# The recurrent layer's mixing weights split during the feed-forward layer before it and kept in DRAM; two elementwise steps on other engines

## The chip, the cores and the metric

One core of a Trainium2 chip runs the whole program. The metric is device time in microseconds (us) from the first to the last instruction of one execution, with what the runtime puts around it; the median of three runs is compared.

## What is computed

Two blocks of two layers each act on 512 tokens of width 1024. The change touches the second block: its first feed-forward layer (width 2816) and the recurrent layer after it (`odd_mixer`). Cut to those:

```python
def swiglu(x, w_gate, w_up, w_down):
    return (silu(x @ w_gate) * (x @ w_up)) @ w_down

def odd_mixer(xn, w_in, w_out, ...):
    z = xn @ w_in                                    # 1024 -> 2048
    h = rglru_mixer(z[..., :1024], ...)
    return (h * gelu(z[..., 1024:])) @ w_out

def rglru_mixer(xb, ...):
    xc = causal_conv(xb, conv_w) + conv_b            # 4 taps
    gate_r = sigmoid(xc @ w_r + b_r)                 # 4 diagonal blocks of 256
    gate_i = sigmoid(xc @ w_i + b_i)
    log_a = -8 * gate_r * softplus(-lam)
    a, mult = exp(log_a), sqrt(-expm1(2 * log_a))
    return scan(h[t] = a[t] * h[t-1] + mult[t] * (gate_i * xc)[t])

for layer in range(2):
    x = x + rms_norm(mixer(rms_norm(x)))             # even_mixer, odd_mixer
    x = x + rms_norm(swiglu(rms_norm(x)))
```

## The kernel before

Activations lie with channels on the 128 partitions and the 512 tokens along the row. Every product is made in three parts: a weight block of 128 outputs by 1024 inputs and the activations are each split into a high half (rounded to the matmul's type) and a low half (the rest), and `product` (L288) adds high by high, high by low and low by high: 24 matmuls of 512 columns a block. `weights` (L269) gets one block: SyncE (SP) starts a load of 512 KB into a raw tile `wp_r`, ScalarE (ACT) copies it into `wp_h`, and a subtraction into `wp_l` runs on VectorE (DVE) unless an engine is named. There are three raw tiles and four of each half. `firsts` (L299) does the first three blocks of a layer together, one half of the tokens at a time, so that it can begin while the norm before it is still running; it splits its weights on GpSimd (POOL).

`ffn` (L1755) runs over 22 pairs of blocks (gate and up), in three groups of 6, 8 and 8. A pair's two products are scaled by the norm (`g_g`, `g_u`), go through Silu, are multiplied on POOL, and are split into `h_h` and `h_l`; after each group come eight blocks of the down weights, and after the last group a norm and the residual (`po_a`, `po_r`, `g_ff`, `res_x`), whose outputs `act_h` and `act_l` the next layer reads.

`odd_mix` (L1646) is the recurrent layer's mixing, in four blocks b of two channel tiles each. `conv(b)` takes two blocks of `w_in` (m = 0 to 7), multiplies by the norm into `xb`, makes the first tap with bias (`ts`, L1677) and adds three taps (`stt`), then splits the result into `o_h` and `o_l`. `gates(b)` multiplies by the block of `w_rg` and takes tanh. `states(b)` makes the decay and the input of the recurrence (`o_mu`, `o_a`, `o_tr`, `o_ti`) and scans it into `o_u`; in it, the product of r0 and i0 runs on POOL. `gate(b)` takes two more blocks of `w_in` (m = 8 to 15) into `o_z`, and `gated(b)` applies gelu, multiplies and splits into `b_h` and `b_l`, which `out_products` (L339) multiplies by the output weights. The blocks for `conv` and the four `w_rg` have their low halves made on POOL, those for `gate` on DVE. The norm of the layer is summed into `res_acc` and needed by the first `xb`.

The text of the kernel gives the order of dependences only: the library that builds the program puts each engine's instructions, and SP's transfers, in a queue of their own, an instruction as early as it reckons its operands and buffers free, ties by the order of the text. Each queue is then carried out strictly in that order.

Of the kernel before, what the change touches and what calls it, by code (L numbers as in the profile page):

```python
# [188 lines left out]
class Prog:  # L189
# [79 lines left out]
    def weights(self, ap, n=1024, eng=None, pool=None):  # L269

        pool = pool or self.wp
        raw = (pool if "r" in pool.tags else self.wp)("r", n)
        self.nc.sync.dma_start(out=raw, in_=ap)
        hi, lo = self.parts_of(pool, n)
        self.copy(hi, raw)
        self.sub(lo, raw, hi.bitcast(F32), eng)
        return hi, lo
# [1368 lines left out]
    def odd_mix(self, es, B):  # L1646
        nc, tc, xs, r = self.nc, self.tc, self.xs, self.rr
        A = Alloc(es, tc, "o7", {
            "sp2": (1, 8), "hb": (1, 16), "h": (4, L), "l": (4, L), "xb": (2, L + 3), "xc": (2, 1024),
            "tr": (2, 1024), "ti": (2, 1024), "a": (2, L), "mu": (2, L), "u": (2, 1024), "z": (2, 1024),  # L1650
        })
        ps = self.psum(mm=4, g=4)

        sp = self.sp
        sp2, hb = A("sp2"), A("hb")
        self.ts(sp2, sp, 2.0, ALU.mult)
        self.ts(hb[:, 0:8], self.vec("rg_b_r"), 0.5, ALU.mult)
        self.ts(hb[:, 8:16], self.vec("rg_b_i"), 0.5, ALU.mult)
        cw, cb = self.vec("rg_cw"), self.vec("rg_conv_b")

        def proj(m, eng=None):
            if m in first:
                return first[m][0]
            w = self.weights(self.I["w_od"][m], eng=eng or nc.gpsimd)
            px = ps("mm")
            self.product(px, w, xs, X)
            return px

        def conv(b):
            c2, parts = A("xc"), []  # L1670
            for i in range(2):
                m = 2 * b + i
                px = proj(m)
                xb, c = A("xb"), c2[:, i * L:(i + 1) * L]
                nc.gpsimd.memset(xb[:, 0:3], 0.0)
                self.mul(xb[:, 3:], px, r)
                self.ts(c, xb[:, 3:], cw[:, 4 * m + 3:4 * m + 4], ALU.mult, cb[:, m:m + 1], ALU.add)  # L1677
                for j in range(3):
                    self.stt(c, xb[:, j:j + L], cw[:, 4 * m + j:4 * m + j + 1], c, ALU.mult, ALU.add)
                parts.append(self.split(A, c))  # L1680
            return c2, parts

        us, ys = {}, []

        def gates(b, c2, parts):
            w = self.weights(self.I["w_rg"][b], eng=nc.gpsimd)
            tr, ti = A("tr"), A("ti")
            for i in range(2):
                m, s = 2 * b + i, slice(i * L, (i + 1) * L)
                for g, t in enumerate((tr, ti)):  # L1690
                    p = ps("g")
                    self.product(p, w, parts, X, k0=4 * g + 2 * i)
                    self.act(t[:, s], p, ACT.Tanh, scale=0.5, bias=hb[:, 8 * g + m:8 * g + m + 1])
            return tr, ti

        def states(b, c2, tr, ti):


            h, ts = A("u"), []
            for i in range(2):  # L1700
                m, s = 2 * b + i, slice(i * L, (i + 1) * L)
                u, w = A("mu"), A("a")
                self.act(u, tr[:, s], ACT.Tanh, scale=sp[:, m:m + 1], bias=sp[:, m:m + 1])
                self.act(w, tr[:, s], ACT.Exp, scale=sp2[:, m:m + 1], bias=sp2[:, m:m + 1])
                nc.scalar.activation(out=w, in_=w, func=ACT.Copy, scale=0.5, bias=0.5)
                ts.append((s, tr[:, s], ti[:, s], u, w))
            for s, r0, i0, u, w in ts:
                self.act(r0, u, ACT.Sqrt, scale=-1.0)
                self.stt(u, u, -1.0, w, ALU.add, ALU.mult)
                self.stt(w, u, 2.0, w, ALU.add, ALU.mult)  # L1710
                self.stt(i0, i0, 1.0, c2[:, s], ALU.add, ALU.mult)
                self.mul(r0, r0, i0, nc.gpsimd)
                self.mul(r0, r0, w)
                self.ts(w, w, 2.0, ALU.mult, -1.0, ALU.add)
                nc.vector.tensor_tensor_scan(out=h[:, s], data0=w, data1=r0, initial=0.0, op0=ALU.mult, op1=ALU.add)
            us[b] = h

        def gate(b):
            z = A("z")
            for i in range(2):  # L1720
                px = proj(8 + 2 * b + i, nc.vector)
                self.mul(z[:, i * L:(i + 1) * L], px, r)
            return z

        def gated(b, z, cuts):
            self.act(z, z, ACT.Gelu_apprx_tanh)
            hi, lo = self.parts_of(B)
            for s in cuts:
                self.mul(z[:, s], us[b][:, s], z[:, s])
                self.copy(hi[:, s], z[:, s])  # L1730
                self.sub(lo[:, s], z[:, s], hi[:, s].bitcast(F32))
            ys.extend((hi[:, s], lo[:, s]) for s in halves)

        halves, whole = (slice(0, L), slice(L, 2 * L)), (slice(0, 2 * L),)
        first = dict(enumerate(self.firsts(ps, [self.I["w_od"][m] for m in range(3)], xs)))
        self.rms(ps("g"))
        cs, zs = {0: conv(0), 1: conv(1)}, {}
        for b in range(3):
            t = gates(b, *cs[b])
            zs[b] = gate(b)  # L1740
            if b == 2:
                t3 = gates(3, *cs[3])
            states(b, cs[b][0], *t)
            if b < 2:
                cs[b + 2] = conv(b + 2)
            if b:
                gated(b - 1, zs[b - 1], whole)
        states(3, cs[3][0], *t3)
        zs[3] = gate(3)
        gated(2, zs[2], whole)  # L1750
        gated(3, zs[3], halves)
        return ys


    def ffn(self, l, last=None):  # L1755

        nc, tc, xs, r = self.nc, self.tc, self.xs, self.rr
        with ExitStack() as es:
# [5 lines left out]
            def proj(m):  # L1764
                w = self.weights(self.I[f"w_gu{l}"][m])
                px = ps("mm")
                self.product(px, w, xs, X)
                return px

            first = [px for px, _ in self.firsts(ps, [self.I[f"w_gu{l}"][m] for m in range(3)], xs)]  # L1770
            first.append(proj(3))
            self.rms(ps("z"))
            for a, b in ((0, 6), (6, 14), (14, 22)):
                hs = []
                for i in range(a, b):
# [11 lines left out]
                    self.copy(hi, t[0])  # L1787
                    self.sub(lo, t[0], hi.bitcast(F32))
                    hs.append((hi, lo))
                if l == a == 0:  # L1790
                    self.softplus()
                n = (b - a) * 128
                block = lambda m: self.I[f"w_d{l}"][m][:, a * 128:b * 128]
                if b < 22:
                    for m in range(8):
# [5 lines left out]
                        else:  # L1801
                            self.add(ff[m], ff[m], px)
                else:
                    pre, stats = (last, None) if last else self.prenorm(es, ps, "norm_mix_pre", l + 1)
                    use, done = self.postnorm(es, ps, "norm_ffn_post", l, pre, ff, last)
                    self.out_products(ps, block, hs, PARTS[:2], use, done, n=n, keep=4 if last else 3, spare=(H, 2))
# [65 lines left out]
```

## Time and profile before

| | us |
|---|---|
| median of 3 runs | 2132.29 (2127.01 to 2133.92) |
| the profiled execution | 2134.38 |
| its span, first to last instruction | 2132.6 |
| PE busy in it | 2045.8 (96%) |
| DVE, ACT, POOL busy | 1349.8, 911.0, 427.0 |

The second block's first feed-forward layer reads its first weights at about 1153 and runs to about 1560; the recurrent mixing goes on from there to about 1715, its output product to about 1750. Times in the trace are counted from the span's start. A line such as L250 is a helper's (`tt`), so steps are told apart by their tiles: `o_` are those of the recurrent mixing, `g_` and `h_` of the feed-forward layer, `wp_` weights, `po_` a norm after a product. PE is TensorE. An arrow `<-` in a wait names what ended it.

### The profile page before, as it was taken

The page shows a single profiled execution, that of the slowest core. Times are in us where ns is not written, and L with a number is a line of the kernel's source. Part 1 is how long each engine was busy: PE and PEld are TensorE (multiplying, and loading weights), DVE is VectorE, ACT ScalarE, POOL GpSimd, SP SyncE. Part 2 cuts the span into 40 slices and gives each one's busy share as a digit, 9 for nine tenths or more (in the row PEclk, how much of TensorE's full clock was granted, in tenths as well). Part 3 has the DMA queues.
Part 4 walks back from the last instruction along what each step waited for, and adds up shares of the span by engine and source line. Part 5 has one row for each costly group of instructions (what it writes and reads, how often), then busy time and mean ns, then how long its engine had stood idle before and what let it go on. Part 6 is the DMA issues. An engine that isn't in the chain of part 4 may idle for free.

```text
span 2132.6 us, 29872 instructions
## 1 busy us (share of the span) xinstructions
PE 2045.8 (96%) x11624; PEld 1740.2 (82%) x11624; DVE 1349.8 (63%) x2290; ACT 911.0 (43%) x1634; POOL 427.0 (20%) x403
## 2 busy tenths in 40 slices
PE   6999999999999999989999999999989799999997
PEld 4888888889888888888778888888877588888886
DVE  6775566786666665786665734535589886254455
ACT  2563343445433444455655533222356645322231
POOL 1111111354122221042112310101143322010011
PEclk9999999999999999999989999999999899999998
DMA  8344442321111111224423133333312232333231
GB/s 300 119 158 136 146 142 71 116 88 60 50 54 56 50 50 50 89 85 158 119 70 99 60 96 102 99 98 93 116 50 69 70 99 80 109 96 93 98 109 40
DMA packets 80142, 204.97 MB, mean 96 GB/s; under 512 B 19200, under 2 KB 28160, under 8 KB 80000
## 3 DMA queue, kind: packets, MB, share of 16 engines
q1 hardware_dynamic: 80000, 203.06, 30.1%
q8 instruction: 91, 1.49, 0.3%
q14 instruction: 51, 0.42, 0.1%
HBM read 188.87 MB, written 14.16 MB: 95 GB/s over the span
## 4 chain that ended last, share of the span: by engine, by line
PE 76%; DVE 13%; issue 5%; ACT 4%; POOL 1%; DMA 1%; SPq 0%; POOLq 0%; DVEq 0%; ACTq 0%
PE mm L313 56%; PE a L313 5%; PE mc L313 3%; PE x L313 2%; PE S L313 2%; DVE res_x L266 1%; PE s L313 1%; PE pt L651 1%; PE o L313 1%; DVE wp_l L250 1%; PE mc L425 1%; DVE o_xc L266 1%; DVE n_a L250 1%; ACT wp_h L244 1%; PE z L313 1%
## 5 line engine op out<-in xcount | busy, mean ns | idle before, releaser
L244 ACT ACTIVATE wp_h<-wp_r 128x1024 fp32r<-128x1024 f32 (+2 forms) x263 | 271.3, 1037 | 456.1 <-PE mm L313 263.4
L250 DVE TENSOR_TENSOR wp_l<-wp_r,wp_h 128x1024 fp32r<-128x1024 f32 (+1 forms) x236 | 326.9, 1388 | 108.7 <-ACT wp_h L244 108.6
L313 PE MATMUL mm<-act_h,wp_l 128*128 128x512 f32 (+1 forms) x1008 | 379.4, 376 | 12.0 <-DVE wp_l L250 10.2
L313 PE MATMUL mm<-act_l,wp_h 128*128 128x512 f32 (+1 forms) x1008 | 380.0, 377 | 1.9 <-POOL act_l L250 1.9
L313 PE MATMUL mm<-act_h,wp_h 128*128 128x512 f32 (+1 forms) x1008 | 379.8, 377 | 1.7 <-ACT wp_h L244 1.3
L313 PE MATMUL mm<-a_h,wp_h 128*128 128x512 f32 (+1 forms) x920 | 336.8, 367 | 5.5 <-ACT wp_h L244 3.3
L313 PE MATMUL mm<-a_h,wp_l 128*128 128x512 f32 (+1 forms) x920 | 329.8, 359 | 1.2 <-POOL wp_l L250 1.2
L313 PE MATMUL mm<-a_l,wp_h 128*128 128x512 f32 (+1 forms) x920 | 328.6, 358 | 0.9 <-DVE a_l L250 0.9
L313 PEld LDWEIGHTS mm<-act_h,wp_l 128*128 128x128 f32 x1008 | 194.0, 192 | 46.4 <-DVE wp_l L250 11.1
L313 PEld LDWEIGHTS mm<-act_l,wp_h 128*128 128x128 f32 x1008 | 193.6, 192 | 35.9 <-POOL act_l L250 2.6
L313 PEld LDWEIGHTS mm<-act_h,wp_h 128*128 128x128 f32 x1008 | 193.5, 192 | 34.7 <-ACT wp_h L244 1.8
L313 PEld LDWEIGHTS mm<-a_h,wp_h 128*128 128x128 f32 x920 | 174.1, 189 | 30.6 <-ACT wp_h L244 3.3
L313 PEld LDWEIGHTS mm<-a_l,wp_h 128*128 128x128 f32 x920 | 174.1, 189 | 25.9 <-issue 1.9
L313 PEld LDWEIGHTS mm<-a_h,wp_l 128*128 128x128 f32 x920 | 173.8, 189 | 24.6 <-POOL wp_l L250 1.4
L250 POOL TENSOR_TENSOR g_g<-g_g,g_u 128x512 f32<-128x512 f32 x44 | 61.1, 1390 | 549.3 <-DVE g_u L250 502.9
L313 PE MATMUL mm<-h_l,wp_h 128*128 128x512 f32 (+1 forms) x344 | 129.2, 376 | 0.6 <-DVE h_l L250 0.5
L313 PE MATMUL mm<-h_h,wp_h 128*128 128x512 f32 (+1 forms) x344 | 129.0, 375 | 0.3 <-ACT h_h L244 0.3
L313 PE MATMUL mm<-h_h,wp_l 128*128 128x512 f32 (+1 forms) x344 | 128.8, 374 | 0.0
L250 DVE TENSOR_TENSOR g_u<-mm,res_rr 128x512 f32<-128x512 f32 x44 | 30.4, 690 | 125.9 <-PE mm L313 125.9
L250 POOL TENSOR_TENSOR wp_l<-wp_r,wp_h 128x1024 fp32r<-128x1024 f32 x27 | 69.4, 2574 | 135.9 <-ACT wp_h L244 119.0
L244 ACT ACTIVATE m_km<-m_k 128x512 f32<-128x512 f32 x56 | 37.5, 672 | 122.9 <-DVE m_k L250 101.4
L247 ACT ACT_TABLE_LOAD x60 | 77.0, 1283 | 1.8 <-PEq L1860 0.7
(496 smaller groups left out, 3927.3 us busy)
## 6 DMA issues: line engine op xcount, KB each, us to landing
wp_r<-w_gu SPq DMA_DIRECT2D x88, 512.0 KB, 3.5
wp_r<-w_c SPq DMA_DIRECT2D x40, 512.0 KB, 3.5
wp_r<-wada SPq DMA_DIRECT2D x32, 512.0 KB, 3.7
wp_r<-w_d SPq DMA_DIRECT2D x32, 512.0 KB, 3.6
wp_r<-w_ab SPq DMA_DIRECT2D x26, 512.0 KB, 4.8
st_r<-wada SPq DMA_DIRECT2D x16, 512.0 KB, 7.9
wp_r<-w_od SPq DMA_DIRECT2D x16, 512.0 KB, 3.5
s_d<-s_s SPq DMA_DIRECT2D x24, 256.0 KB, 2.4
```

What stands on the lines that cost most here:

```text
L244: self.nc.scalar.activation(out=out, in_=in_, func=ACT.Copy, scale=scale)
L247: self.nc.scalar.activation(out=out, in_=in_, func=func, **kw)
L250: (eng or self.nc.vector).tensor_tensor(out=out, in0=a, in1=b, op=op)
L266: self.nc.vector.scalar_tensor_tensor(out=out, in0=a, scalar=s, in1=b, op0=op0, op1=op1)
L313: self.nc.tensor.matmul(out=out, lhsT=a, rhs=b, start=start, stop=stop)
L425: self.nc.tensor.matmul(out=p[32 * k:32 * k + 32, :], lhsT=self.sc[:, 4 * j + k, :], rhs=raw[j][:, k * 256:(k + 1) * 256], start=j == 0, s ...
L651: nc.tensor.transpose(pt[:, i * 128:(i + 1) * 128], P[h][:, i * 128:(i + 1) * 128], self.idn)
```

## The change

A new generator `odd_weights` makes the split halves of the 16 blocks of `w_od` and the four of `w_rg` in a pool of its own, two tiles of each kind, and stores both halves in a DRAM tensor of 20 by 2 by 512 KB. `ffn(0)` takes one step of it after each pair of products, so that 20 of its 22 pairs have one, and closes the pool in the last group ahead of the output product. The halves are made on ACT and DVE. `weights`, given a pair of DRAM halves, starts two loads straight into `wp_h` and `wp_l` and splits nothing; the recurrent mixing's `firsts`, `proj` and `gates` all do so. The product of r0 and i0 moves from POOL to DVE, and the first tap with its bias from DVE to ACT. The output weights `wo_od` are loaded and split as before.

```diff
@@ -269,6 +269,11 @@
     def weights(self, ap, n=1024, eng=None, pool=None):
 
         pool = pool or self.wp
+        if isinstance(ap, tuple):
+            w = self.parts_of(pool, n)
+            for t, part in zip(w, ap):
+                self.nc.sync.dma_start(out=t.bitcast(F32), in_=part)
+            return w
         raw = (pool if "r" in pool.tags else self.wp)("r", n)
         self.nc.sync.dma_start(out=raw, in_=ap)
         hi, lo = self.parts_of(pool, n)
@@ -1658,10 +1663,10 @@
         self.ts(hb[:, 8:16], self.vec("rg_b_i"), 0.5, ALU.mult)
         cw, cb = self.vec("rg_cw"), self.vec("rg_conv_b")
 
-        def proj(m, eng=None):
+        def proj(m):
             if m in first:
                 return first[m][0]
-            w = self.weights(self.I["w_od"][m], eng=eng or nc.gpsimd)
+            w = self.weights(self.od[m])
             px = ps("mm")
             self.product(px, w, xs, X)
             return px
@@ -1674,7 +1679,7 @@
                 xb, c = A("xb"), c2[:, i * L:(i + 1) * L]
                 nc.gpsimd.memset(xb[:, 0:3], 0.0)
                 self.mul(xb[:, 3:], px, r)
-                self.ts(c, xb[:, 3:], cw[:, 4 * m + 3:4 * m + 4], ALU.mult, cb[:, m:m + 1], ALU.add)
+                self.act(c, xb[:, 3:], ACT.Identity, scale=cw[:, 4 * m + 3:4 * m + 4], bias=cb[:, m:m + 1])
                 for j in range(3):
                     self.stt(c, xb[:, j:j + L], cw[:, 4 * m + j:4 * m + j + 1], c, ALU.mult, ALU.add)
                 parts.append(self.split(A, c))
@@ -1683,7 +1688,7 @@
         us, ys = {}, []
 
         def gates(b, c2, parts):
-            w = self.weights(self.I["w_rg"][b], eng=nc.gpsimd)
+            w = self.weights(self.rg[b])
             tr, ti = A("tr"), A("ti")
             for i in range(2):
                 m, s = 2 * b + i, slice(i * L, (i + 1) * L)
@@ -1709,7 +1714,7 @@
                 self.stt(u, u, -1.0, w, ALU.add, ALU.mult)
                 self.stt(w, u, 2.0, w, ALU.add, ALU.mult)
                 self.stt(i0, i0, 1.0, c2[:, s], ALU.add, ALU.mult)
-                self.mul(r0, r0, i0, nc.gpsimd)
+                self.mul(r0, r0, i0)
                 self.mul(r0, r0, w)
                 self.ts(w, w, 2.0, ALU.mult, -1.0, ALU.add)
                 nc.vector.tensor_tensor_scan(out=h[:, s], data0=w, data1=r0, initial=0.0, op0=ALU.mult, op1=ALU.add)
@@ -1718,7 +1723,7 @@
         def gate(b):
             z = A("z")
             for i in range(2):
-                px = proj(8 + 2 * b + i, nc.vector)
+                px = proj(8 + 2 * b + i)
                 self.mul(z[:, i * L:(i + 1) * L], px, r)
             return z
 
@@ -1732,7 +1737,7 @@
             ys.extend((hi[:, s], lo[:, s]) for s in halves)
 
         halves, whole = (slice(0, L), slice(L, 2 * L)), (slice(0, 2 * L),)
-        first = dict(enumerate(self.firsts(ps, [self.I["w_od"][m] for m in range(3)], xs)))
+        first = dict(enumerate(self.firsts(ps, self.od[:3], xs)))
         self.rms(ps("g"))
         cs, zs = {0: conv(0), 1: conv(1)}, {}
         for b in range(3):
@@ -1751,6 +1756,18 @@
         gated(3, zs[3], halves)
         return ys
 
+    def odd_weights(self, es):
+
+        Z = Alloc(es, self.tc, "z8", {"r": (2, 1024), "h": (2, 1024), "l": (2, 1024)}, side="right")
+        d = self.dram.tile([20, 2, 128, 1024], F32, name="od_d")
+        blocks = [self.I["w_od"][m] for m in range(16)] + [self.I["w_rg"][b] for b in range(4)]
+        parts = [(d[i, 0], d[i, 1]) for i in range(20)]
+        self.od, self.rg = parts[:16], parts[16:]
+        for i in (0, 1, 2, 3, 16, 8, 9, 4, 5, 17, 10, 11, 6, 7, 18, 19, 12, 13, 14, 15):
+            for t, part in zip(self.weights(blocks[i], pool=Z), parts[i]):
+                self.nc.sync.dma_start(out=part, in_=t.bitcast(F32))
+            yield
+
 
     def ffn(self, l, last=None):
 
@@ -1770,6 +1787,8 @@
             first = [px for px, _ in self.firsts(ps, [self.I[f"w_gu{l}"][m] for m in range(3)], xs)]
             first.append(proj(3))
             self.rms(ps("z"))
+            e1 = es.enter_context(ExitStack())
+            ahead = iter(()) if last else self.odd_weights(e1)
             for a, b in ((0, 6), (6, 14), (14, 22)):
                 hs = []
                 for i in range(a, b):
@@ -1787,6 +1806,7 @@
                     self.copy(hi, t[0])
                     self.sub(lo, t[0], hi.bitcast(F32))
                     hs.append((hi, lo))
+                    next(ahead, None)
                 if l == a == 0:
                     self.softplus()
                 n = (b - a) * 128
@@ -1801,6 +1821,9 @@
                         else:
                             self.add(ff[m], ff[m], px)
                 else:
+                    for _ in ahead:
+                        pass
+                    e1.close()
                     pre, stats = (last, None) if last else self.prenorm(es, ps, "norm_mix_pre", l + 1)
                     use, done = self.postnorm(es, ps, "norm_ffn_post", l, pre, ff, last)
                     self.out_products(ps, block, hs, PARTS[:2], use, done, n=n, keep=4 if last else 3, spare=(H, 2))
```

## Rows read from the trace of the kernel before

**Rows 1.** page, part 1: busy us of each engine (share of the span) xinstructions

```profile
PE 2045.8 (96%) x11624; PEld 1740.2 (82%) x11624; DVE 1349.8 (63%) x2290; ACT 911.0 (43%) x1634; POOL 427.0 (20%) x403
```

**Rows 2.** stretches: length, busy of PE PEld DVE ACT POOL, clock, DMA share, GB/s

```profile
1190.00:1515.00 325.00, 322.42 (x1463) 268.16 (x1464) 160.38 (x168) 107.49 (x147) 42.45 (x34) 0.99 0.31 95
1555.00:1580.00 25.00, 20.91 (x151) 20.34 (x149) 20.73 (x37) 15.43 (x35) 14.54 (x17) 0.86 0.07 23
...
1580.00:1715.00 135.00, 112.17 (x460) 87.98 (x459) 121.27 (x129) 79.19 (x100) 43.77 (x25) 0.94 0.24 77
```

**Rows 3.** what PE waited for, 1555 to 1720: us in total, times, longest

```profile
PE mm L313 <- DVE wp_l L250: 10.2, 2, 10.0
PE z L313 <- DVE po_a L250: 4.1, 1, 4.1
PE g L313 <- DVE res_acc L250: 3.9, 1, 3.9
PE g L313 <- ACT o_h L244: 2.4, 2, 2.0
PE g L313 <- DVE o_l L250: 1.9, 2, 1.7
PE mm L313 <- POOL wp_l L250: 1.8, 1, 1.8
PE mm L313 <- ACT wp_h L244: 1.3, 1, 1.3
PE mm L313 <- DVE b_l L250: 1.3, 1, 1.3
```

**Rows 4.** order of time, the long wait: start us, us, engine, line, operation

```profile
1678.14 4.51 DVE L266 SCALAR_TENSOR_TENSOR o_a<-o_mu,o_a 128x512 f32<-128x512 f32 x2
1687.31 2.33 DVE L250 TENSOR_TENSOR wp_l<-wp_r,wp_h 128x1024 fp32r<-128x1024 f32 x2
...
1688.55 0.79 PE L313 MATMUL mm<-act_h,wp_l 128*128 128x512 f32 x1 [9.96 <-DVE wp_l L250]
1693.69 0.39 PE L313 MATMUL mm<-act_h,wp_l 128*128 128x512 f32 x1
```

**Rows 5.** DVE by line, 1580 to 1715: xcount, busy us, mean ns

```profile
L266 DVE SCALAR_TENSOR_TENSOR o_xc<-o_xb,vecs,o_xc 128x512 f32<-128x512 f32 x24 | 21.7, 922 | 0.1
L266 DVE SCALAR_TENSOR_TENSOR o_a<-o_mu,o_a 128x512 f32<-128x512 f32 x8 | 13.8, 1730 | 0.1
L250 DVE TENSOR_TENSOR o_tr<-o_tr,o_a 128x512 f32<-128x512 f32 x8 | 11.9, 1501 | 0.0
L250 DVE TENSOR_TENSOR wp_l<-wp_r,wp_h 128x1024 fp32r<-128x1024 f32 x9 | 10.7, 1211 | 0.0
L263 DVE TENSOR_SCALAR o_xc<-o_xb,vecs 128x512 f32<-128x512 f32 x8 | 8.3, 1052 | 0.0
```

**Rows 6.** order of time: a DVE step alone and beside POOL

```profile
1619.45 0.68 DVE L266 SCALAR_TENSOR_TENSOR o_a<-o_mu,o_a 128x512 f32<-128x512 f32 x1
...
1643.50 5.60 POOL L250 TENSOR_TENSOR wp_l<-wp_r,wp_h 128x1024 fp32r<-128x1024 f32 x2
...
1646.78 2.88 DVE L266 SCALAR_TENSOR_TENSOR o_a<-o_mu,o_a 128x512 f32<-128x512 f32 x1
```

**Rows 7.** order of time: the norm before the recurrent layer

```profile
1558.11 2.71 POOL L250 TENSOR_TENSOR wp_l<-wp_r,wp_h 128x1024 fp32r<-128x1024 f32 x1 [1.91 <-ACT wp_h L244]
...
1558.65 2.45 DVE L266 SCALAR_TENSOR_TENSOR res_x<-g_ff,vecs,res_x 128x256 f32<-128x256 f32 x1
```

**Rows 8.** a copy in the feed-forward layer, the first mixer's stretch, page part 6

```profile
1427.68 1.06 ACT L244 ACTIVATE wp_h<-wp_r 128x1024 fp32r<-128x1024 f32 x1 [4.38 <-PE mm L313]
...
80.00:400.00 320.00, 318.81 (x2260) 272.39 (x2260) 205.38 (x559) 150.39 (x380) 45.38 (x54) 1.00 0.41 131
...
wp_r<-w_od SPq DMA_DIRECT2D x16, 512.0 KB, 3.5
s_d<-s_s SPq DMA_DIRECT2D x24, 256.0 KB, 2.4
```

## The prediction

> **What bounds the kernel now.** I read the busy shares of the page first. TensorE (PE) is busy for 2045.8 of 2132.6 us [rows 1], so some 87 us of idle is all that any change can win, unless it shortens products, which this one does not. So the second view is a table of stretches, to find where that idle is [rows 2]. The feed-forward layer ahead of the change (1190 to 1515) has PE busy for 322.4 of 325 us: full. The recurrent layer's mixing (1580 to 1715) has it busy for 112.2 of 135, with VectorE (DVE) busy for 121.3 and GpSimd (POOL) for 43.8: here DVE, not PE, is nearly full. The stretch between (1555 to 1580) has 20.9 of 25 at a granted clock of 0.86. Third, the list of what PE waited for from 1555 to 1720 [rows 3]: 26.9 us in eleven waits. 13.3 of them are for split weights: 10.2 for the low halves made by DVE, 1.8 for those by POOL, 1.3 for the high halves of ScalarE (ACT). Then 4.3 for the convolution's halves o_h and o_l, 3.9 for the sum of squares res_acc, 4.1 for po_a of the norm before, 1.3 for b_l.
>
> The long wait in order of time [rows 4]: DVE is in the states from 1678.14 on, two of its instructions alone take 4.51 us, and only at 1687.31 does it come to two low halves; PE starts again at 1688.55. It then runs at the low clock: to 1693.69, with 12 matmuls, it takes 5.14 us, where a matmul takes 0.22 in a full stretch (322.4 us by 1463) [rows 2], 2.6 for 12. So 2.5 us more belong to this wait.
>
> Why DVE is so full is seen by the same instruction on both sides [rows 5, 6]. The o_a step takes 0.68 us at 1619.45 and 2.88 at 1646.78, where POOL is in a run of low halves (1643.50, 5.60 us). Instructions of both engines do not run beside each other at full speed.
>
> **The change part by part.** *Removed from the recurrent layer*: 20 copies on ACT (1.06 us, the like in rows 8, so 21), 8 low halves on DVE (1.21 [rows 5], so 9.7), 12 low halves and 8 products r0*i0 on POOL, where only the small memsets and the output weights stay. *Moved*: 8 first taps from DVE (8.3 us [rows 5]) to ACT, at no more there than a copy twice as wide, 1.06; 8 products to DVE at 0.68 each (5.4), the time of a step of this shape alone [rows 6]. *Relieved*: with POOL gone, o_a falls from 1.73 to 0.68, o_tr from 1.50 to about 0.68 (8 each: 8.4 and 6.6), and 24 taps from 0.92 to about 0.74 (4.4; 0.74 is my estimate from the 0.68 of o_a). DVE then has 121.3 - 9.7 - 8.3 + 5.4 - 19.4 = 89 us of work in the stretch, against PE's 112: PE is the bound again.
>
> What each wait becomes [rows 3]:
> - Split weights, 13.3 us: gone whole, since PE now waits for a transfer alone. The low clock behind the long one, 2.5, goes with it.
> - po_a, 4.1: POOL makes a low half at 1558.11 (2.71 us), and the DVE step at 1558.65, ahead of po_a, takes 2.45 [rows 7]; alone it would need some 0.5. I take 2.0, and 1.0 for the clock behind it (0 to 2.5: 20.9 us at 0.86 bound it [rows 2]).
> - res_acc, 3.9: the same meeting with POOL's low half of the fourth block. I take 2.0; the rest is the chain of sum, root and three steps, which stays.
> - o_h and o_l, 4.3: the taps get shorter, but the first now goes from DVE to ACT and back. I take 3.0. What is queued behind a tap on ACT are the other half's o_h and the gates' activations; ACT loses 21 us and gets at most 8.5.
> - b_l, 1.3: 0.6, the end of the states being relieved too.
>
> Sum: 13.3 + 2.5 + 3.0 + 2.0 + 3.0 + 0.6 = 24.4 us.
>
> *Added ahead*, in the feed-forward layer: 20 times a load, a copy (1.06), a low half (1.21) and two stores of 512 KB, one after each of the first 20 pairs of products. ACT goes from 107.5 to 129 of 325 us, DVE from 160.4 to 185. The transfers add 20 x 1.5 MB, so 31 MB: 95 GB/s at a share of 0.31 become about 190 at 0.62. I cost all that at 1 us. The cover is the weights' lead: a copy starts when a product has ended [rows 8] and frees one of four buffers, so three products of 24 matmuls (5.3 us each) lie between it and its use; less copy and low half, some 13 us. Three raw buffers give as much again ahead of it. A store waits on the SP queue for its half, and the next layer of loads is queued behind it; a wait of one copy and one low half is 2.3 us, well inside the lead. If that cover is gone, a held load shows on PE at 1.06 + 1.21 + 3.5 (landing of a load) + 1.06 = 6.8 us a time [rows 8]. The nearest precedent has the same form: from 80 to 400, 24 stores of 256 KB to DRAM stand among the loads on SP, and PE is busy for 318.8 of 320 us [rows 8]. Where the lead is not built up, behind the norm at 1190 to 1225, up to five of the new low halves (1.21 each; 35 us at some 7 us a block) can stand ahead of the norm's steps: the bound is 0 to 6, no gain being possible where PE is full, and 1 is nearer the precedent.
>
> *Added in the recurrent layer*: each block now comes as two loads straight into the buffers that PE reads, so a load can be issued only when PE has finished the block four earlier, and the loads queued behind it on SP (the next blocks', then the output weights') wait with it. One takes 3.5 us to land [rows 8], two at most 7, against the three products of lead, 16 us. Only at 1580, where three buffers come free at once, must PE take what lands: the fourth block covers 5.4 us of it. For this and for queues that come out in a new order I charge 3 us (0 to 8; the nearest rows are PE's shorter waits of 1.3 to 2.4 in rows 3, of which four would make 8; what could be gained is in the sum already).
>
> Weighed against the notes: what rows 6 show is a step that takes four times as long beside a POOL instruction. The Trainium skill (SBUF — State Buffer, section "SBUF: two separate sides") says that VectorE and GpSimd hold one pair of ports as a lock, for a whole instruction, when VectorE has two inputs in SBUF. That speaks against the added half: each of the 20 new low halves can shut GpSimd out for its length and be shut out itself. By that rule the feed-forward layer would pay at the two ends of its hidden blocks, where GpSimd's product is awaited soonest, an estimate of 2 x 2.4 us; it stays inside the bound of 6 above. The trace bears the rule out by 2.88 against 0.68.
>
> **The forecast.** Net 24.4 - 1 - 3 = 20.4 us off the profiled execution's 2134.4, so 2114.0. The median of the three runs is 2.1 below the profiled one, 2132.3; I carry half of that and forecast 2113. The spans of the costs (0 to 6 and 0 to 8, not both at their ends), and of the shares that I took of the other waits, make it 2104 to 2121.
>
> **The rivals.**
> *The recurrence takes the waits' place* (0.14). The states still follow one another: gates, activations with table loads, DVE steps, scan, gating. If PE waits on o_h, o_l and b_l for as long as before and half of the weights' 15.8 turns into waits for them, the gain is about 8: 2126. For it: DVE was 90% busy and its steps are strictly in order. Against it: 89 us of work in some 115.
> *Everything goes* (0.06): the 26.9 us, the low clock behind them (2.5 and up to 2.5) and no cost at all, 32 off: 2102.
> *The change does not do what it says* (0.05): the first loads of the recurrent layer wait for stores that came late, or the queues come out so that PE waits as before: within a few us of 2132. Against it: the last block is due two pairs before the end of the layer.
> *Slower: SP holds the feed-forward layer's loads behind the stores* (0.09). Were the queue strictly in the order of the text, each store would wait for a copy that stands behind its pair's last product, and the next pair's loads would be issued after it: 6.8 us of PE idle a block, 136 for 20, so 2250. It decides from four blocks on: 27 us, against a gain of 20.4 and the 6.4 that can be told. Against it is the precedent of rows 8, where stores stand among the loads and PE idles for 1.2 us in 320.
>
> **How the numbers follow.** A measurement of this kernel can tell some 0.3%, 6.4 us, from no change. The forecast has a chance of 0.66, the rivals 0.14, 0.06, 0.05 and 0.09. Faster by more than 0.3% (below 2125.9): 0.66 + 0.06 + 0.09 of the first rival = 0.81. Within: 0.05 + 0.05 = 0.10. Slower: 0.09. The range goes from 2104 to 2128: it takes in most of the first rival and leaves out the second, the slower one and little else.
>
> **What would show it.** Right: no PE wait on weights between 1555 and 1720 but for loads; the recurrent mixing some 18 us shorter, with PE above 95%; o_a and o_tr near 0.7 us; the feed-forward layer as long as before within 3 us, its DMA share about doubled. Wrong: PE waits on wp_h or wp_l in the feed-forward layer, or SP waits of over 10 us ahead of a store; in the recurrent layer, PE waits for o_h, o_l or for loads that add up to over 12 us.

## The result, and the profile after

The changed kernel takes 2110.99 us (median of 4 runs, 2109.53 to 2118.35) against 2131.19 for the kernel before on the same chip: a ratio of 0.9915, 95% interval 0.9899 to 0.9932, so 20 us faster. The profiled execution took 2109.53, its span 2107.7, 24.9 us less than before.

Page, part 1, after: as much DVE work as before less 15 us, POOL 45 us less [rows 1].

```profile
PE 2038.4 (97%) x11624; PEld 1736.8 (82%) x11624; DVE 1335.0 (63%) x2302; ACT 918.5 (44%) x1642; POOL 382.4 (18%) x383
```

**Where the time went.** Each of the last four layers ends in a norm whose sum of squares PE starts with a matmul `z<-po_a`. The first of these matmuls marks the layer's end. Here are the marks of before, then those of after (start us, us, engine, line, operation):

```profile
1178.65 0.70 PE L313 MATMUL z<-po_a,ones 128*128 128x256 f32 x2
...
1547.16 0.70 PE L313 MATMUL z<-po_a,ones 128*128 128x256 f32 x2
...
1741.29 0.70 PE L313 MATMUL z<-po_a,ones 128*128 128x256 f32 x2
...
2107.41 0.70 PE L313 MATMUL z<-po_a,ones 128*128 128x256 f32 x2
```

```profile
1176.29 0.70 PE L318 MATMUL z<-po_a,ones 128*128 128x256 f32 x2
...
1547.90 0.70 PE L318 MATMUL z<-po_a,ones 128*128 128x256 f32 x2
...
1715.71 0.70 PE L318 MATMUL z<-po_a,ones 128*128 128x256 f32 x2
...
2083.04 0.70 PE L318 MATMUL z<-po_a,ones 128*128 128x256 f32 x2
```

The feed-forward layer ahead went from 1547.16 - 1178.65 = 368.5 to 371.6, so 3.1 longer; the recurrent layer from 194.1 to 167.8, so 26.3 shorter; the layer after it is 1.2 longer, the tail 0.5 shorter, and 2.4 had been gained before the first mark, where nothing was changed. Together -24.9. The lengths of the feed-forward and of the recurrent layer are what every experiment below is measured by.

Stretches after (length, busy of PE, PEld, DVE, ACT, POOL, clock, DMA share, GB/s), to be held against [rows 2]; the third line is the mixing alone, for the experiments:

```profile
1190.00:1515.00 325.00, 321.11 (x1459) 267.01 (x1457) 178.58 (x185) 124.84 (x162) 42.91 (x33) 0.99 0.54 188
...
1580.00:1715.00 135.00, 133.78 (x609) 109.61 (x610) 106.26 (x139) 82.44 (x108) 16.18 (x12) 0.99 0.48 167
...
1580.00:1690.00 110.00, 108.78 (x463) 87.80 (x464) 87.72 (x119) 69.49 (x91) 8.57 (x9) 0.98 0.46 163
```

In the mixing PE is now the full engine, 99% busy instead of 83, at a granted clock of 0.99 instead of 0.94, and 609 matmuls fall into the stretch where 460 did. (The end of this stretch now reaches into the output product, so only the share, not DVE's sum, is to be compared.) All that PE waits for between 1555 and 1720, against 26.9 us [rows 3]:

```profile
PE g L318 <- DVE res_acc L250: 3.1, 1, 3.1
PE z L318 <- DVE po_a L250: 2.6, 1, 2.6
```

Between the marks of the recurrent layer PE's idle time went from 27.0 to 5.8 us, which is 21.2 of the 26.3. The other 5.1 is time in which PE is busy: the same 823 matmuls took 167.1 us at a mean granted clock of 0.94 and 162.0 at 0.98.

DVE by line, 1580 to 1715 (count, busy us, mean ns): o_a fell from 1730 to 682 ns, o_tr from 1501 to 872, the taps from 922 to 746 [rows 5].

```profile
L266 DVE SCALAR_TENSOR_TENSOR o_xc<-o_xb,vecs,o_xc 128x512 f32<-128x512 f32 x24 | 17.5, 746 | 1.6 <-ACT o_xc L247 1.3
L250 DVE TENSOR_TENSOR o_tr<-o_tr,o_a 128x512 f32<-128x512 f32 x8 | 7.0, 872 | 0.0
L266 DVE SCALAR_TENSOR_TENSOR o_a<-o_mu,o_a 128x512 f32<-128x512 f32 x8 | 5.5, 682 | 0.0
```

**What was paid.** In the feed-forward layer the price is at its beginning. PE's waits from 1185 to 1205 before, then after, and DVE in the same norm after, in order of time:

```profile
PE z L313 <- DVE po_a L250: 1.8, 1, 1.8
PE mm L313 <- POOL act_l L250: 0.5, 1, 0.5
```

```profile
PE mm L318 <- ACT act_h L244: 2.1, 1, 2.1
PE z L318 <- DVE po_a L250: 1.7, 1, 1.7
PE mm L318 <- POOL act_l L250: 1.2, 1, 1.2
```

```profile
1190.25 1.50 DVE L250 TENSOR_TENSOR z_l<-z_r,z_h 128x1024 fp32r<-128x1024 f32 x1 [0.19 <-ACT z_h L244]
1191.67 0.41 DVE L266 SCALAR_TENSOR_TENSOR po_t<-z,po_r 128x256 f32<-128x256 f32 x1
1192.12 0.51 DVE L266 SCALAR_TENSOR_TENSOR po_t<-po_t,po_r 128x256 f32<-128x256 f32 x1
1192.56 1.76 DVE L250 TENSOR_TENSOR z_l<-z_r,z_h 128x1024 fp32r<-128x1024 f32 x1
1194.24 0.41 DVE L266 SCALAR_TENSOR_TENSOR po_r<-po_t,po_r 128x256 f32<-128x256 f32 x1
```

Two halves of the blocks split ahead (`z_l`, 3.26 us together) stand between the steps that make the root, on which act_h and so PE wait. The waits' sum goes from 2.3 to 5.0 us. The text takes the first block after the first pair of products; the library has put two ahead of that, since their operands were free.

### The profile page after: what moved, and what is told of

It reads as the page before. It is cut to its first block, busy times and chain, and to the rows that moved or that the text cites. A ratio compares the mean times of both kernels' runs of the same rounds, so it can differ in the third digit from the quotient of the medians.

```text
span 2107.7 us, 30001 instructions
## 1 busy us (share of the span) xinstructions
PE 2038.4 (97%) x11624; PEld 1736.8 (82%) x11624; DVE 1335.0 (63%) x2302; ACT 918.5 (44%) x1642; POOL 382.4 (18%) x383
## 5 line engine op out<-in xcount | busy, mean ns | idle before, releaser
L244 ACT ACTIVATE wp_h<-wp_r 128x1024 fp32r<-128x1024 f32 (+2 forms) x243 | 250.9, 1037 | 409.9 <-PE mm L318 245.8
L250 DVE TENSOR_TENSOR wp_l<-wp_r,wp_h 128x1024 fp32r<-128x1024 f32 (+1 forms) x228 | 319.6, 1404 | 100.2 <-ACT wp_h L244 100.1
L318 PEld LDWEIGHTS mm<-a_h,wp_l 128*128 128x128 f32 x920 | 174.3, 189 | 24.0 <-issue 0.7
L318 PEld LDWEIGHTS mm<-h_l,wp_h 128*128 128x128 f32 x344 | 64.8, 188 | 13.5 <-DVE h_l L250 2.1
```

The source lines that it names most:

```text
L244: self.nc.scalar.activation(out=out, in_=in_, func=ACT.Copy, scale=scale)
L250: (eng or self.nc.vector).tensor_tensor(out=out, in0=a, in1=b, op=op)
L318: self.nc.tensor.matmul(out=out, lhsT=a, rhs=b, start=start, stop=stop)
```

## The experiments

Two theories were put against each other, in the expectations below. *Weights*, the prediction's main term: PE gained because it no longer waits for halves that are made in the engines' queues. *Relief*: GpSimd's instructions with two inputs made VectorE slow, and their leaving pays, wherever the weights come from. The prediction had the second as a part of the sum; it had not asked whether it would do by itself.

Times are in us. Two columns of this table are lengths between the marks above, from the one profiled execution of each run; the last is POOL's busy time in the table of stretches, 1580 to 1690. Ratios are to the kernel before on the same chip.

| run | median us | ratio (95% interval) | feed-forward | recurrent | POOL |
|---|---|---|---|---|---|
| before | 2131 | 1 | 368.5 | 194.1 | 35.2 |
| c1_changed | 2110.24 | 0.9906 (0.9889 to 0.9924) | 374.7 | 167.6 | 8.5 |
| e1_split_only | 2114.73 | 0.9927 (0.9911 to 0.9943) | 372.4 | 174.3 | 22.9 |
| e2_moves_only | 2122.67 | 0.9966 (0.9953 to 0.9978) | 368.5 | 186.6 | 25.5 |
| e3_ahead_only | 2134.89 | 1.002 (1.001 to 1.003) | 371.8 | 193.9 | 35.6 |
| e4_late_start | 2104.86 | 0.9885 (0.9869 to 0.9901) | 368.5 | 168.1 | 8.6 |
| e5_one_block | 2104.64 | 0.9874 (0.9855 to 0.9893) | 370.0 | 167.8 | 8.5 |
| e6_pool_leaves | 2108.15 | 0.9891 (0.9875 to 0.9908) | 368.5 | 170.7 | 12.4 |
| e7_twice | 2115.51 | 0.9928 (0.9912 to 0.9945) | 378.8 | 167.8 | 10.3 |
| e8_halves_only | 2115.81 | 0.9934 (0.9922 to 0.9946) | 368.5 | 178.9 | 23.4 |
| e9_pool_busy | 2127.94 | 0.9988 (0.9978 to 0.9998) | 372.8 | 185.4 | 33.2 |
| e10_late_no_pool | 2098.17 | 0.9851 (0.9836 to 0.9866) | 368.7 | 168.1 | 0.5 |
| e11_simple_no_pool | 2100.40 | 0.9856 (0.9836 to 0.9877) | 368.8 | 170.0 | 0.6 |

**The changed kernel again.**

> The changed kernel once more, beside the other runs of its chip. Both theories expect what was measured first, 18 to 20 us below the kernel before (some 2111), with no PE wait on wp_h or wp_l in the recurrent mixing.

2110.24: the same time in the second measurement. Its feed-forward layer is 6.2 us longer than before, where the first profile had 3.1, so the price ahead is 3 to 6. The waits in the norm are the same in both. What differs is one wait behind it: at 1262.92 PE waits 1.7 us for a hidden half (h_h), where the first profile has 0.3, and from 1255 to 1275 the granted clock is 0.91 where the first profile has 1.00.

**The two halves of the change.** e1 undoes the moves; e2 has them alone. Shown is e1 against the changed kernel; e2 is the reverse of it, against the kernel before (arguments shortened to `...`).

```diff
-                self.act(c, xb[:, 3:], ACT.Identity, scale=..., bias=...)
+                self.ts(c, xb[:, 3:], ..., ALU.mult, ..., ALU.add)
...
-                self.mul(r0, r0, i0)
+                self.mul(r0, r0, i0, nc.gpsimd)
```

> The changed kernel with both moved steps put back: POOL makes the product r0*i0, DVE the first tap; the split weights still come from DRAM. Theory of the weights (PE waited for halves that stood in DVE's and POOL's queues, and those halves are gone): nearly the whole gain stays, 16 to 20 us off, some 2113, and PE has no wait on weights; DVE is busier by 8.3 us of taps and by steps that meet POOL's eight products, but stays below PE. Theory of the relief (DVE was slowed by POOL, and POOL leaving its stretch is what pays): o_a and o_tr stay at 1.3 us or more, and at least 6 us of the gain are lost, some 2119, as PE waits on o_h, o_l and b_l.

> The kernel before with the two moved steps alone: r0*i0 on DVE, the first tap on ACT; weights are split in place as before. Theory of the weights: DVE's queue is shorter by some 3 us of work and 10 of relief, but low halves still stand in it behind the states; 3 to 8 us off, some 2126, and the waits on wp_l stay at 6 us or more in sum. Theory of the relief: half of the meetings go, 10 us or more off, 2121 or less.

The split alone brings 0.73%, the moves alone 0.34%; the recurrent layer is 19.9 us shorter by the one, 7.5 by the other, 26.5 by both. They all but add up. By the numbers set beforehand these two runs speak for *weights* rather than for *relief*: e1 loses 4.5 us of the gain, nearer to the 4 at most of *weights* than to the 6 at least of *relief*; e2 gains 7.4, inside of the 3 to 8 of *weights*, where *relief* asked for 10. PE's long wait for DVE's low half is 6.9 us in e2 instead of 10.0; with it DVE in order of time, first before, then in e2:

```profile
PE mm L313 <- DVE wp_l L250: 6.9, 1, 6.9
```

```profile
1686.17 1.21 DVE L1715 TENSOR_TENSOR_SCAN o_u<-o_a,o_tr 128x512 f32<-128x512 f32 x1
```

```profile
1677.74 1.21 DVE L250 TENSOR_TENSOR wp_l<-wp_r,wp_h 128x1024 fp32r<-128x1024 f32 x1
...
1680.35 1.21 DVE L1715 TENSOR_TENSOR_SCAN o_u<-o_a,o_tr 128x512 f32<-128x512 f32 x1
```

Each low half is made on the engine that made it before, but not at the same place in its queue: before, the awaited one (1687.31 [rows 4]) stood behind both scans; in e2 the library has put it ahead of the second. So this shorter wait doesn't tell the theories apart. Nor do the times alone: e1 takes the weights out of the queues, but it takes 12 low halves off POOL as well.

**The price ahead.** e3 makes the 20 blocks in the feed-forward layer and uses none; the recurrent layer is that of before. Its edit is the kernel before with `odd_weights` and the lines in `ffn` that step and close it; shown are two of them:

```diff
+            ahead = iter(()) if last else self.odd_weights(e1)
...
+                    next(ahead, None)
...
```

> The kernel before with the added side alone: all 20 blocks are split during the feed-forward layer and stored, and nothing reads them; the recurrent layer splits its weights in place as before. If the added side costs what the stretch between the two norms shows (3 us longer in the changed kernel), 2 to 4 us more than before, some 2134, with the extra PE waits in the norm at the layer's start alone. If stores held back the feed-forward layer's loads, PE would wait on wp_h there, 7 us a time.

It costs 3.3 us by the medians and 3.3 between the marks (371.8 against 368.5). PE's waits in the norm are those of the changed kernel, to the tenth:

```profile
PE mm L313 <- ACT act_h L244: 2.1, 1, 2.1
...
PE mm L313 <- POOL act_l L250: 1.2, 1, 1.2
```

e4 is the changed kernel with the first two loads ahead held until the norm's root is done, by a write into their tiles that reads it:

```diff
+            raw = Z("r")
+            if i < 2:
+                self.nc.vector.tensor_copy(out=raw[:, 0:1], in_=self.rr[:, 0:1])
+            self.nc.sync.dma_start(out=raw, in_=blocks[i])
...
```

> The changed kernel, but the first two loads of the blocks made ahead wait for the feed-forward layer's norm to be done, so that none of their copies and low halves stands in the norm's chain. If those are what the feed-forward layer pays (PE there waits 2.1 us on act_h and 1.2 on act_l in the changed kernel, 0.5 before), 2 to 3 us less than the changed kernel, some 2108, with the norm's PE waits back at 1.8 and 0.5. If it pays by the transfers or by SP's queue all along the layer, the time stays as that of the changed kernel, 2111, or rises, since the same transfers are packed into less time.

The layer is back at 368.5, and the kernel at 2104.86, 5.4 below the changed one. The waits of its norm (1185 to 1205) are the short ones again:

```profile
PE z L318 <- DVE po_a L250: 1.7, 1, 1.7
PE mm L318 <- POOL act_l L250: 1.4, 1, 1.4
PE mm L318 <- ACT act_h L244: 0.4, 1, 0.4
```

So most of the price is the place of the first two blocks; the wait for a hidden half that c1 has at 1262.92 is gone in e4 too. Two more runs asked about the rest of the work ahead. e5 is e4 with one block made ahead and read 20 times, so it leaves out the other 19; e7 is the changed kernel with every copy and low half ahead made twice. Of both edits the main lines:

```diff
-        parts = [(d[i, 0], d[i, 1]) for i in range(20)]
+        parts = [(d[0, 0], d[0, 1])] * 20
```

```diff
+            for _ in range(2):
+                self.copy(hi, raw)
+                self.sub(lo, raw, hi.bitcast(F32))
```

> The recurrent side alone: one block is split ahead, behind the norm, and read 20 times in place of 20 different ones, so that 19 loads, splits and pairs of stores are left out (the recurrent layer computes with one block's weights throughout). Weights come from DRAM by the same 40 loads. If the added side costs 3 us and only by standing in the norm's chain, this is 2 to 4 us below the changed kernel and equal to the kernel with the late start, some 2108. If the transfers of 30 MB cost something all along the layer too, it is below that one by what they cost.

> The changed kernel with every copy and low half of the blocks ahead made twice: 21 us more on ACT and 24 more on DVE in the feed-forward layer, no transfer more. If that work is covered by PE there, the time rises by no more than the copies that stand in the norm's chain, 0 to 4 us, some 2113. If ACT's and DVE's work in the layer shows on PE, 10 us or more, 2121 and above, with PE waits on wp_h and wp_l.

e5 is where e4 is (2104.64): behind the norm the other 19 blocks, 19 x 1.5 = 29 MB of transfers, cost nothing that can be told. e7 is 5 us slower than the changed kernel, between its two expectations (up to 4, or 10 and more), and one wait of PE has that size; it is the wait that has 1.7 us in c1. Before it, in order of time: a copy of a block ahead waits for its load, its low half on DVE waits for the copy, and g_u, of which the awaited hidden half is made, stands behind that low half.

```profile
1262.55 1.06 ACT L244 ACTIVATE z_h<-z_r 128x1024 fp32r<-128x1024 f32 x1 [1.96 <-DMA z_r<-w_rg]
1263.64 1.23 DVE L250 TENSOR_TENSOR z_l<-z_r,z_h 128x1024 fp32r<-128x1024 f32 x1 [2.18 <-ACT z_h L244]
1264.78 0.69 DVE L250 TENSOR_TENSOR g_u<-mm,res_rr 128x512 f32<-128x512 f32 x1
...
1268.16 0.72 PE L318 MATMUL mm<-h_h,wp_h 128*128 128x512 f32 x1 [4.79 <-ACT h_h L244]
```

The cover of the work ahead is real but not deep: 20 copies and 20 low halves more (1.06 [rows 8] and 1.21 us [rows 5], so 45) found a place where it was gone, and the changed kernel is close to it.

**Without the weights in DRAM.** e6 is e2, and DVE makes all low halves of the recurrent layer's weights, in its own queue; nothing is split ahead. Shown are two of its lines. The low halves new on DVE are the 12 that GpSimd made, not 15 as the expectation says.

```diff
-            w = self.weights(self.I["w_od"][m], eng=eng or nc.gpsimd)
+            w = self.weights(self.I["w_od"][m])
...
-            w = self.weights(self.I["w_rg"][b], eng=nc.gpsimd)
+            w = self.weights(self.I["w_rg"][b])
```

> The kernel before with the two moved steps and with all the recurrent layer's low halves made on DVE, none on POOL; weights are split in place, nothing comes from DRAM. DVE gets 15 more low halves (1.21 us each) and meets POOL no more. Theory of the relief: o_a, o_tr and the taps fall to 0.7 us, and 12 us or more of the gain appear, 2119 or less. Theory of the weights: DVE has about as much work as before (some 112 us of 135) and all of the low halves stand in its queue, behind states and taps; 0 to 8 us off, 2123 to 2131, and PE waits on wp_l by DVE for 6 us or more.

2108.15, as fast as the changed kernel. DVE now has more of the weights' work than before, and PE's waits for it are 2.4 us where they were 10.2 [rows 3]. PE's waits for low halves (1555 to 1720), and the stretch of mixing with DVE 93% busy:

```profile
PE mm L313 <- DVE wp_l L250: 2.4, 2, 1.2
...
PE mm L313 <- POOL wp_l L250: 0.6, 1, 0.6
```

```profile
1580.00:1690.00 110.00, 106.78 (x458) 85.81 (x458) 102.16 (x133) 82.02 (x104) 12.43 (x9) 0.99 0.29 95
```

Without DRAM the recurrent layer gets 23.5 of the 26.5 us. e8 has the low halves on DVE but leaves the two moved steps where they were:

> The kernel before, with every low half of the recurrent layer's weights (w_od and w_rg) made on VectorE instead of 12 of them on GpSimd; the product of r0 and i0 stays on GpSimd, the first tap on VectorE, and nothing goes to DRAM. Theory 'weights' (what PE gained, it gained because it no longer waits for halves in the engines' queues): VectorE gets 12 x 1.21 = 14.5 us more to do in its own queue, so the waits for wp_l stay at 10 us or more: 2131, or up to 10 slower. Theory 'relief' (GpSimd's instructions with two inputs were what made VectorE slow): 12 of 20 such instructions go, VectorE gives 14.5 us and gets back what its o_a and o_tr lost beside them; e6 had 22 less than the kernel before and e2 8 less, so most of the 14 between them: 2118 to 2124, with one or two PE waits over 2 us left where r0*i0 still meets a step.

2115.81, 15.2 below the kernel before, more than *relief* had asked for, though DVE got 12 low halves more to make. With 12 of 20 POOL instructions gone the recurrent layer is 178.9; the eight products that stay keep o_a at 1741 ns, o_tr<-o_tr,o_a is down at 952:

```profile
L266 DVE SCALAR_TENSOR_TENSOR o_a<-o_mu,o_a 128x512 f32<-128x512 f32 x8 | 13.9, 1741 | 0.1
...
L250 DVE TENSOR_TENSOR o_tr<-o_tr,o_a 128x512 f32<-128x512 f32 x8 | 7.6, 952 | 0.0
```

The runs so far make a chain for the recurrent layer, each link one edit: POOL's low halves to DVE take it from 194.1 to 178.9 (e8), the two moves to 170.7 (e6), the weights from DRAM to 167.6 (c1). The last link, 3.1 us, is of a like size without the moves: 178.9 in e8, 174.3 in e1, which differ by the DRAM weights alone. No run parts the two moves, so how much of their 8.2 us is POOL's product and how much the tap that DVE no longer makes stays open.

**With the weights in DRAM, and POOL busy.** e9 is the changed kernel with 17 subtractions on POOL whose result nobody reads. In the traces the order of PE's, DVE's and ACT's instructions, and of SP's transfers, is that of the changed kernel, operation by operation, so no step has anything new ahead of it but on POOL. In the recurrent layer no wait of DVE is for POOL, and none of SP's is for the new subtractions.

```diff
+                self.sub(A("idle", 768), w[0][:, :768].bitcast(F32), w[1][:, :768].bitcast(F32), nc.gpsimd)
```

> The changed kernel, with 17 subtractions of 128x768 on GpSimd in the recurrent layer, one for each block behind the first three, that read the block's two halves and write a tile that nobody reads: some 35 us of GpSimd, as much as it had between 1580 and 1690 in the kernel before. PE still takes its weights from DRAM and waits for none of it. Theory 'weights': only the few steps that meet cost something, and PE has halves in hand: at most 4 us slower than the changed kernel, 2111 to 2115. Theory 'relief': o_a, o_tr and the taps are back at 0.9 to 1.7 us, VectorE is some 15 us fuller, and PE waits for o_h, o_l and b_l: 6 to 15 us slower, 2117 to 2126.

2127.94, 17.7 us slower than the changed kernel and 3 from the kernel before: worse than *relief* had asked for, and outside of what *weights* allowed. (The profiled execution, 2123.76, is one of the shortest of its 12.) In order of time, POOL and DVE where the output weights are split:

```profile
1690.94 0.68 DVE L250 TENSOR_TENSOR o_tr<-o_tr,o_a 128x512 f32<-128x512 f32 x1
1691.51 5.45 POOL L250 TENSOR_TENSOR wp_l<-wp_r,wp_h 128x1024 fp32r<-128x1024 f32 x2 [16.91 <-ACT wp_h L244]
1691.55 0.68 DVE L266 SCALAR_TENSOR_TENSOR o_a<-o_mu,o_a 128x512 f32<-128x512 f32 x1
1692.15 2.58 DVE L263 TENSOR_SCALAR o_a<-o_a 128x512 f32<-128x512 f32 x1
...
1694.64 2.85 DVE L250 TENSOR_TENSOR o_tr<-o_tr,o_ti 128x512 f32<-128x512 f32 x1
```

PE's waits, 1555 to 1720; the longest is for ACT's copy of an output weight, at 1691:

```profile
PE mm L318 <- ACT wp_h L244: 7.3, 1, 7.3
PE g L318 <- DVE res_acc L250: 3.5, 1, 3.5
PE z L318 <- DVE po_a L250: 2.6, 1, 2.6
PE g L318 <- ACT o_h L244: 2.0, 2, 1.8
```

That copy stands on ACT behind the third block's b_h, and b_h behind the activations of the fourth block's states, which came late: b_h starts at 1689.44, 143.3 us after the layer's mark, where c1 has 125.8 (1675.60). No row of these waits is for a weight that came from DRAM: the DRAM weights did what they were meant to do, and two thirds of the layer's gain was lost all the same (185.4 against 167.6). *Weights* falls as the main cause.

**POOL out of more places.** e10 is e4, e11 is e6, and in both DVE makes the low halves of the first three blocks of every layer and of every output product.

```diff
-        ws = [self.weights(b, eng=self.nc.gpsimd) for b in blocks]
+        ws = [self.weights(b) for b in blocks]
...
```

> e4_late_start (the changed kernel with the first two loads ahead held until the norm is done), and GpSimd also makes no low halves for the first three blocks of any layer and of any output product: VectorE makes them. If relief is what pays wherever VectorE is on the way to PE, the norms at 1190 and 1555 shorten by 1 to 2 us each, and so at the other layers: 2095 to 2103 against e4's 2104.9. If at these places VectorE is itself the last to be ready, its three more halves (1.21 each) stand ahead of the norm's steps: 2105 to 2112.

> e6_pool_leaves (no DRAM, low halves of the recurrent layer on VectorE) with the same step as e10: VectorE makes the low halves of the first three blocks everywhere. The same two answers: 2098 to 2106 if the norms are relieved, 2108 to 2114 if VectorE is the last there. Against e10 it also says what the 20 blocks split ahead are worth once GpSimd is out of the way: by 'weights' at least 10 us, by 'relief' at most 5.

2098.17 and 2100.40: both beat both kernels, by 12 and 10 us against the changed one (2110.24), 33 and 31 against the one before. The feed-forward and the recurrent layer hardly move, so the gain over e4 and e6 (6.7 and 7.8) is not at the norms at 1190 and 1555, where the expectation had put it too. In the profiles it lies ahead of the first mark, in layers that the change did not touch: PE's idle time there is 37.5 us in e10 against 41.0 in e4, and 35.2 in e11 against 40.7 in e6. The rest of e10's lead can be the clock: e5's first mark comes 6.5 us ahead of e4's with nothing changed before it, at a granted clock of 0.98 from 1080 to the mark, where e4 has 0.91 and e10 0.96. Which steps of those layers gain is not shown. One against the other, they are equal within their intervals: with POOL out of the way the 20 blocks in DRAM are worth 1.9 us between the marks (168.1 against 170.0) and nothing that the medians can tell. e11 has no DRAM tensor, no work ahead and two fifths less DMA traffic in the mixing (92 against 156 GB/s, last column). First e11, then e10:

```profile
1580.00:1690.00 110.00, 107.43 (x465) 86.57 (x464) 100.00 (x137) 84.36 (x108) 0.60 (x6) 1.00 0.30 92
```

```profile
1580.00:1690.00 110.00, 109.19 (x473) 88.47 (x472) 87.20 (x122) 74.75 (x96) 0.50 (x5) 1.00 0.46 156
```

## Why the prediction was right, and where not

The time was right, 2113 against 2111, and the sum by stages roughly so: 24.4 - 3 = 21.4 off the recurrent layer, where 26.3 went, and 1 in the layer ahead, where 3.1 (6.2 in c1) was paid. That the time came out this close is in part luck: the profiled execution lost 24.9 us against a forecast of 20.4, the medians 20.2, and the largest term carries a cause that is not the main one.

- **Split weights, 13.3, and the clock behind them, 2.5.** The waits are gone, as forecast. "PE now waits for a transfer alone" is not the main reason. In e6 the low halves stay in DVE's queue, 12 of them new there, and of these waits 3.0 us are left (2.4 for DVE's, 0.6 for POOL's); in e9 the weights come from DRAM and 17.8 us of the layer are lost again. The rows had both readings in them [rows 4, 6]: of the 4.51 us of two o_a steps ahead of the long wait, 4.51 - 2 x 0.68 = 3.15 are the meeting with POOL. The prediction used that for DVE's sum and not for the wait. How the 10.0 us of this one wait divide between slow steps and the low half's place in the queue is not shown, since the place moved in e2, e6 and e8 as well.
- **Relief of DVE.** Right: o_a at 0.68 (forecast 0.68), the taps at 0.75 (0.74); o_tr at 0.87 (0.68), since POOL still makes the first output weights' halves: one step of 2.25 us at 1662.33 meets the one at 1661.59. The rule that was weighed against the rows is that of the Trainium skill (SBUF — State Buffer, section "SBUF: two separate sides"): the two engines hold one pair of ports as a lock, for a whole instruction. The trace of e9 agrees, where DVE's steps end 0.5 us after the POOL instruction that they met. What the prediction drew from it for the feed-forward layer, that the new low halves would shut POOL out, is not where that layer paid: POOL is busy there (1190 to 1515) for 42.9 us, 42.5 before [rows 2], and the price is the place of two low halves on DVE itself (e3, e4).
- **po_a and res_acc.** Forecast 2.0 off each, with 1.0 for the clock. They lost 1.5 and 0.8; 2.6 and 3.1 are left though POOL makes no low half of the mixing's weights any more, more than the chain of dependent steps was given.
- **o_h, o_l, b_l.** All 5.6 us went, forecast 3.6. The first tap on ACT took 810 ns, under the 1.06 allowed, and the way there and back costs DVE 1.3 us of waiting and PE none. The low clock was forecast at 3.5 in all and gave back 5.1.
- **Work ahead, 1 (0 to 6).** 3 to 6: mis-sized, and over the 3 us that the prediction allowed as a sign of being right. Most of it comes by the mechanism that set the upper bound, low halves that stand ahead of the norm's steps; 1 was taken from a precedent elsewhere in the kernel, and this price was at the one place that the prediction had named as an exception. The rest of the cover held in e4 and e5; in c1 one hidden half came 1.7 us late.
- **Direct loads and new queue orders, 3 (0 to 8).** Nothing: no PE wait for a load from DRAM between 1555 and 1720, and e4's mixing has PE busy for 109.88 of 110 us.
- **SP behind its stores.** SP did wait ahead of its stores in the feed-forward layer, up to 12.5 us (33.0 in 13 waits), which the prediction had named as a sign of going wrong:

```profile
SPq L1768 <- ACT z_h L244: 33.0, 13, 12.5
```

PE felt next to none of it: its waits from 1205 to 1545 add up to 0.6 us. The sign should have been a PE wait for a copy, not a wait of SP.

Of the rivals, *the recurrence takes the waits' place* is what e9 brings about: the same layer with PE fed from DRAM and DVE slow. In the changed kernel it didn't happen because POOL's work left together with the weights.

## What to carry to other kernels

When a full engine's step takes 0.7 us in one place and 2.9 in another, look for what runs on the other engine at that moment before moving work away from the full one: giving VectorE 12 more subtractions, and taking them from GpSimd, made this layer 15 us shorter. A wait that names a weight or a queue can be the slowness of all that stands ahead in it; two experiments help to tell it apart, one that removes the neighbour and leaves the queue, one that restores the neighbour and keeps the queue's order. Work put into a layer's cover belongs behind the norm that opens it, and must be tied there, since a queue takes it as early as its operands are free.

## What the runs showed of the hardware

- In e9 DVE's steps waited for the end of the POOL instruction that they met, and then ran. POOL's two low halves at 1691.51 in e9 took 5.45 us, 2.73 each. The two DVE steps that met them took 2.58 and 2.85 us, and each ends 0.5 us after the POOL instruction beside it (1694.73 against 1691.51 + 2.73, 1697.49 against 1691.51 + 5.45).
- POOL can be the one that is held. In e6 two of its low halves took 7.79 us from 1674.60 on, 2.3 more than in e9. When they began DVE was in a run of steps that kept their own lengths (0.69 us at 1674.63, 0.42 at 1675.24, 0.69 at 1675.57, 1.22 at 1676.17); only the next one, at 1677.31, took 2.82.
- A DVE step with one tensor input is held too: `o_a<-o_a`, 2.58 us in e9 against 0.42 at 1675.67 in the same trace.
- A DVE step that takes one of its two operands from PE's product is not: `o_xb<-mm,res_rr` took 0.68 us at 1596.28 in e9, inside of a POOL subtraction (1596.12, 1.95 us). In the kernel before, with POOL busy for 43.8 of 135 us [rows 2], the eight steps of this form took 0.68 us in the mean, where o_a took 1.73 [rows 5].
- The recurrent layer's length goes along with how long POOL is busy from 1580 to 1690 (the table): 33 to 36 us of POOL with 185 to 194 us, 23 to 26 with 174 to 187, under 13 with 168 to 171. From 12.4 to 0.5 little more is won there, since PE is full.
